# Modulation weights in halves with their four products together, a bank for the value block's last turn, and the turn of dt one z block later

## The chip, the cores and the metric

The kernel runs on one core of one Trainium2 chip. The metric is device time in microseconds (us). The kernel before was run three times: 1810.01, 1811.7 and 1812.62 us, median 1811.7.

## The reference

A two-layer backbone over 1024 latent tokens and 256 context tokens of width 1024, in float32. Layer 0 feeds one projection into a bidirectional RG-LRU and a differential attention with four heads; layer 1 is a bidirectional Mamba-2 (SSD). Around each layer stands an adaptive modulation, and that is what most of the change is about:

```python
def modulation(cvec, w, b):                      # w: 1024 x 3072, one per layer
    m = jax.nn.silu(cvec) @ w + b
    return jnp.split(m, 3, axis=-1)
...
sh, sc, gt = modulation(c, w_mod[i], b_mod[i])   # latent tokens
sh_c, sc_c, gt_c = modulation(c_ctx, w_mod[i], b_mod[i])   # context tokens
u_lat = rms_norm(h_lat, g_pre[i]) * (1.0 + sc[:, None]) + sh[:, None]
...
h_lat = h_lat + gt[:, None] * rms_norm(y_lat, g_post[i])
```

So two vectors, silu(c) and silu(c_ctx), are multiplied by a 1024 x 3072 matrix in each layer. The shift and scale (the first 2048 columns) are needed ahead of a layer, the gate (the last 1024) behind it.

## The kernel before

**Engines and order.** Each engine works through its own instructions in order. A planner sorts each engine's instructions ahead of time, by the order of the program and by its own estimate of when things are ready. `tc.issue_after(x)` adds an edge to it: what is inside the block comes behind x on its engine. TensorE runs everything that is a product; ScalarE (ACT) and VectorE (DVE) empty its PSUM banks; loads are issued from SP's and ScalarE's queues. Float32 products are made exact enough by splitting both operands in a high and a low part, so each projection matmul comes three times (wh x uH, wl x uH, wh x uL: `proj`, L321). A projection block is 128 output columns of a weight by 1280 tokens, in slices of 512, 512 and 256 tokens, 72 matmuls.

**The modulation products.** The two silu vectors stand as the first two of 32 columns of `silu_c` (the rest is zero), eight k tiles of 128. For each k tile there are four products, j = 0 to 3, each of 512 weight columns, into partitions 32j to 32j+31 of one PSUM bank; the profile shows such a float32 product as two matmul records. Three places do this:

- `modulation` (L135) for layer 0, at the start of the kernel: in two passes of 256-column products; the weights of a k tile come in one load of 512 KB that holds all four products' columns.
- `gate_rows` (L187): the gate columns of both layers. Each of the four products of a k tile has a weight tile and a load of its own (256 KB, 2 KB per partition), from a pool `wmod1` of five such buffers. Afterwards the four rows (two silu vectors each) go through the same steps one after the other: VectorE copies the row from PSUM (L199), loads b_mod's part (L203, issued by ScalarE's queue), adds it, loads g_post's part into the same kind of buffer, multiplies (L204), and stores the row to memory (L205, SP's queue). Row and b_mod/g_post parts have one buffer each (tags `u` and `gbm`).
- `modulation` for layer 1: the same with 512-column products, four loads of 256 KB per k tile from the same pool; then ScalarE copies the bank to `mrow` (L165; the buffer with tag `u` of gate_rows), and four transposes turn it.

In program order (L1360 to L1384): LRU block 0's and 1's projections, the scan of block 0, gate_rows, block 2's projections, the scan of block 1, modulation of layer 1, then the weight pool and its small pool close and their memory goes to the rope tables, whose loads (L1366) are issued by ScalarE's queue; then block 3's projections, the scan of block 2, and the first query, gate and key blocks of attention, of which query and key need the rope tables.

**Fills.** `fill` issues matmuls of the identity whose result is not used, behind the last TensorE instruction. `FILL[3]` is 1; it stands in front of the first value transposes.

**The value block's turn.** `v_block` (L471) projects the values of a head and turns ten 128 x 128 tiles by transposes in groups of 4, 4 and 2, each group in a PSUM bank from `c.psum`; for head "0" this pool has two banks, so the third group takes the bank of the first, behind the copy that empties it (L484).

**dt's turn.** In `layer1` (L786) the step sizes dt are worked out by `dt_block`; `turn()` makes the products that transpose and sum them. It stands behind the last matmul of z block 0 (an `issue_after` edge).

Of the kernel before, what the change touches and what calls it, by code (L numbers as in the profile page):

```python
# [10 lines left out]
F32 = mybir.dt.float32  # L11
# [8 lines left out]
P = 128  # L20
D = 1024
KT = 8
# [12 lines left out]
FILL = (5, 1, 1, 1, 1)  # L35
# [96 lines left out]
    return ab  # L132


def modulation(c, a, layer, wpool, tmp, ahead=None, between=None):  # L135
    nc = c.nc
    pcol = 16 if layer == 0 else 93
    gcol = 40 if layer == 0 else 117
    ms = c.cst.tile([P, 16, 2], F32, name=f"ms{layer}")
    g = c.cst.tile([P, KT, 2], F32, name=f"g{layer}")  # L140
    parts = 2 if between else 1
    kn = KT // parts
    nq = kn // 2
    cw = nq * P
    for hf in range(parts):
        pm = c.pm()
        for k in range(KT):
            src = a["w_mod"][layer, k * P : (k + 1) * P, 0 : 2 * D].rearrange("p (s d) -> p s d", s=2)
            cols = []
            if parts == 2:  # L150
                wm = wpool.tile([P, 2, 512], F32, name=f"wm{layer}_{hf}{k}", tag="wm")
                nc.sync.dma_start(wm, src[:, :, 512 * hf : 512 * hf + 512])
                cols = [wm[:, 0, :], wm[:, 1, :]]
            else:
                for j in range(4):
                    wm = wpool.tile([P, cw], F32, name=f"wm{layer}_{j}{k}", tag="wm")
                    nc.sync.dma_start(wm, src[:, j // 2, cw * (j % 2) : cw * (j % 2) + cw])
                    cols.append(wm)
            if ahead:
                ahead(hf, k)  # L160
            for j in range(4):
                w = cols[j // 2][:, cw * (j % 2) : cw * (j % 2) + cw] if parts == 2 else cols[j]
                nc.tensor.matmul(pm[32 * j : 32 * j + 32, 0:cw], c.sc[:, k, :], w, start=(k == 0), stop=(k == KT - 1))
        mrow = tmp.tile([P, 512], F32, name=f"mrow{layer}{hf}", tag="u")[:, 0:cw]
        nc.scalar.copy(mrow, pm[:, 0:cw])  # L165
        pc = c.pm()
        if layer == 0:
            fill(c, pc, FILL[1], cw)
        for q in range(nq):
            nc.tensor.transpose(pc[:, P * q : P * q + P], mrow[:, P * q : P * q + P], c.ident)  # L170
        if layer == 0 and hf == 0:
            c.turned = last_pe(nc)
        pv = pc[:, 0:cw].rearrange("p (q j r) -> p j q r", q=nq, r=32)
        for h in range(2):
            o = 8 * h + kn * hf
            nc.vector.tensor_tensor(ms[:, o : o + kn, :].rearrange("p (j q) s -> p j q s", q=nq), pv[:, 2 * h : 2 * h + 2, :, 0:2],
                                    c.pa[:, pcol + o : pcol + o + kn].rearrange("p (j q) -> p j q", q=nq).unsqueeze(3).to_broadcast([P, 2, nq, 2]), OP.add)
        ks = slice(kn * hf, kn * hf + kn)
        nc.vector.scalar_tensor_tensor(g[:, ks, :], ms[:, 8 + ks.start : 8 + ks.stop, :], 1.0,
                                       c.pa[:, gcol + ks.start : gcol + ks.stop].unsqueeze(2).to_broadcast([P, kn, 2]),  # L180
                                       OP.add, OP.mult)
        if between and hf == 0:
            between(ms, g)
    return ms, g


def gate_rows(c, a, wpool, tmp):  # L187
    nc = c.nc
    pm = c.pm()
    for k in range(KT):  # L190
        for j in range(4):
            w = wpool.tile([P, 512], F32, name=f"wg{j}_{k}", tag="wm")
            o = 2 * D + 512 * (j % 2)
            nc.sync.dma_start(w, a["w_mod"][j // 2, k * P : (k + 1) * P, o : o + 512])
            nc.tensor.matmul(pm[32 * j : 32 * j + 32, :], c.sc[:, k, :], w, start=(k == 0), stop=(k == KT - 1))
    for j in range(4):
        layer, n = j // 2, slice(512 * (j % 2), 512 * (j % 2) + 512)
        row = tmp.tile([P, 512], F32, name=f"grow{j}", tag="u", bufs=1)[0:2, :]
        nc.vector.tensor_copy(row, pm[32 * j : 32 * j + 2, :])  # L199
        for q, src, op in ((0, a["b_mod"][layer : layer + 1, 2 * D + n.start : 2 * D + n.stop], OP.add),  # L200
                           (1, a["g_post"][layer : layer + 1, n], OP.mult)):
            bm = tmp.tile([2, 512], F32, name=f"gbm{j}{q}", tag="gbm", bufs=1)
            nc.scalar.dma_start(bm, src.to_broadcast([2, 512]))  # L203
            nc.vector.tensor_tensor(row, row, bm, op)  # L204
        nc.sync.dma_start(c.grow_d[:, layer, n], row)  # L205

# [17 lines left out]
def last_pe(nc):  # L224
    return next(i for i in reversed(nc.cur_bb.bb.instructions) if i.engine == mybir.EngineType.PE)


def fill(c, ps, n, w=512, behind=None):

    nc = c.nc  # L230
    with c.tc.issue_after(behind or last_pe(nc)):
        for _ in range(n):
            nc.tensor.matmul(ps[:, :w], c.ident, c.ident.unsqueeze(1).to_broadcast([P, w // P, P]), start=True, stop=True)
# [239 lines left out]
def v_block(c, w, uH, uL, pool, apool, name):  # L473
    nc = c.nc
    vt = pool.tile([P, T], F32, name=f"vt_{name}", tag="qf")
    proj(c, w, uH, uL, name, lambda ps, t0, n: nc.scalar.copy(vt[:, t0 : t0 + n], ps))
    v = apool.tile([P, NT, P], F32, name=f"v_{name}", tag="v", bufs=2)
    for j0, n in ((0, 4), (4, 4), (8, 2)):
        ps = c.psum()
        if name == "0" and j0 == 0:  # L480
            fill(c, ps, FILL[3])
        for j in range(n):
            nc.tensor.transpose(ps[:, j * P : (j + 1) * P], vt[:, (j0 + j) * P : (j0 + j + 1) * P], c.ident)
        nc.scalar.copy(v[:, j0 : j0 + n, :], ps[:, : n * P].rearrange("p (j e) -> p j e", e=P))  # L484
    return v
# [304 lines left out]
def layer1(c, a, uH, uL, U, out, dram, h_d, psm, xdt):  # L790
    nc, tc = c.nc, c.tc
# [14 lines left out]
    zp = c.upool  # L806
    nz = 3
    with ExitStack() as s1:
        pool = s1.enter_context(tc.tile_pool(name="p1", bufs=2, side="right"))
        c.wpools = [(U.enter_context(tc.tile_pool(name=f"wst1{i}", bufs=1)), U.enter_context(tc.tile_pool(name=f"wsp1{i}", bufs=1))) for i in range(2)]  # L810
        c.wcyc = 0
        with tc.tile_pool(name="dtp", bufs=1, side="right") as dp:
            tabs, turn = dt_block(c, a, xdt, dp, scst, dr)
            z_block(c, a, 0, uH, uL, zp, dr)
            with tc.issue_after(c.last):
                turn()
        for i in range(1, nz):
            z_block(c, a, i, uH, uL, zp, dr)
        late, store = [None], []

        def block(i, slices, done):
            x = conv_block(c, a, i, uH, uL, pool, slices, late[0])
            late[0] = done(x)

        for g in range(G):
            def done_b(xb, g=g):
                nc.scalar.dma_start(dr["bt"][g], xb[:, 259:XC])
                return lambda: nc.scalar.dma_start(dr["bk"][g], tok_major(c, xb, pool, f"b{g}"))

            def done_c(xc, g=g):  # L830
                nc.scalar.dma_start(dr["ct"][g], xc[:, 259:XC])

            block(16 + g, SL1, done_b)
            block(20 + g, SLAT, done_c)
            for q in range(4):
                def done_x(xs, g=g, q=q):
                    def tok():
                        t = tok_major(c, xs, pool, f"x{4 * g + q}")
                        nc.scalar.dma_start(dr["xk"][g, :, :, q * P : (q + 1) * P].rearrange("c p e -> p c e"), t[:, 2:, :])
                        while store:  # L840
                            store.pop()()
                        store.append(x_states(c, t, 4 * g + q, pool, tabs[0], dr))
                    return tok

                block(4 * g + q, SL1, done_x)
        z_block(c, a, nz, uH, uL, zp, dr)
        with tc.issue_after(c.last):
            late[0]()
        store.pop()()
# [3 lines left out]
    k = ssd_setup(c, a, dr, tabs, S, psm)  # L853
# [5 lines left out]
    for i in range(nz + 1, 16):  # L859
# [4 lines left out]
        n = i - nz - 2  # L864
# [338 lines left out]
def backbone(ctx, tc, a, out):  # L1203
    nc = tc.nc
    c = Ctx()
# [3 lines left out]
    dr = {}  # L1209
# [22 lines left out]
    uH = upool.tile([P, KT, T], F32R, name="u0H")  # L1232
    uL = upool.tile([P, KT, T], F32R, name="u0L")
# [109 lines left out]
    cur = lru_in(c, a, 0, lp, qp, uH, uL, rest)  # L1343
    s4 = ExitStack()
    sp1 = c.sp1
    wm = s4.enter_context(tc.tile_pool(name="wmod1", bufs=5))
    tmp = s4.enter_context(tc.tile_pool(name="mtmp1", bufs=1))
    for i in range(4):
        nxt = lru_in(c, a, i + 1, lp, qp, uH, uL) if i < 3 else None
# [196 lines left out]
```

## Time and profile before

The page is of one profiled execution on the chip. Engines' busy times are shares of its span; the span is the time between its first and last recorded instruction.

| | |
|---|---|
| time of the profiled execution | 1812.95 us |
| its span | 1811.0 us |
| mean granted TensorE clock | 0.991 of full speed |
| TensorE (PE) busy | 97%, 8896 matmuls |
| VectorE (DVE) / ScalarE (ACT) / GpSimd (POOL) busy | 61% / 43% / 20% |
| read / written in device memory | 165.99 MB / 78.92 MB |

A row of a timeline gives the start and length of one instruction or of several alike (x8), its engine, line and operation, the tile that it writes and those that it reads, and in brackets how long the engine stood idle before it and what ended that. PEclk is the granted clock of TensorE as a share of 2.4 GHz. Matmul records overlap, since the array is pipelined: their lengths add up to more than the time that they take.

### The profile page before, as it was taken

Reading aid. Unit: us, or ns where it says so; the run is one execution under the profiler, and the core shown is the slowest. Engines: PE = TensorE matmul, PEld = TensorE weight load, DVE = VectorE, ACT = ScalarE, POOL = GpSimd, SP = SyncE. Lnnn points to the kernel's source line nnn. Section 1 sums busy time; section 2 is a strip of 40 time slices with the busy share of each in tenths; the row PEclk is TensorE's granted clock in tenths of the full one; section 3 lists DMA queues with packets and bytes.
Section 4 is the critical chain, followed back from the end, with each engine's and each line's share of the span. In section 5 each row is a group of like instructions: output and inputs, shape, how many; then the busy total and the mean of one; then the engine's idle time right before and its main releaser. Section 6 shows DMA issues by size and latency. Waiting matters only on the chain.

```text
span 1811.0 us, 24076 instructions
## 1 busy us (share of the span) xinstructions
PE 1753.4 (97%) x8896; PEld 1327.8 (73%) x8896; DVE 1106.3 (61%) x1646; ACT 782.1 (43%) x1571; POOL 369.0 (20%) x423
## 2 busy tenths in 40 slices
PE   6999999999999998999999999999999999999997
PEld 2665377788888887886788888887777566666675
DVE  3735456784837667566746565655111766777797
ACT  4542455374636456444433333334111554343443
POOL 1201000000000000110005242424111443434432
PEclk9999999999999999999999999999999999999999
DMA  7434513432222225342335353546632655656464
GB/s 249 147 97 154 172 64 124 140 86 90 78 75 70 85 53 189 117 140 82 89 121 148 114 145 123 148 124 178 216 105 82 221 194 176 223 193 210 157 206 146
DMA packets 231290, 250.42 MB, mean 138 GB/s; under 512 B 16329, under 2 KB 176078, under 8 KB 231174
## 3 DMA queue, kind: packets, MB, share of 16 engines
q1 hardware_dynamic: 202416, 217.12, 38.5%
q10 hardware_dynamic: 28758, 31.78, 5.5%
q8 instruction: 70, 1.15, 0.3%
q14 instruction: 46, 0.38, 0.1%
HBM read 165.99 MB, written 78.92 MB: 135 GB/s over the span
## 4 chain that ended last, share of the span: by engine, by line
PE 43%; DVE 5%; ACT 2%; issue 1%; DMA 1%; POOL 1%; ACTq 0%; DVEq 0%; SPq 0%; POOLq 0%
PE psap L321 13%; PE pscp L321 11%; PE psap L1119 8%; PE psat L929 3%; PE psdo L1061 2%; PE psdy L1083 2%; PE psda L1050 1%; DVE xbc L350 1%; PE psdy L1078 1%; DVE wl_xb L299 1%; PE psda L1034 1%; PE pscu L747 0%; ACT xp_xb L340 0%; PE psat L1111 0%; ACT tok_x L748 0%
## 5 line engine op out<-in xcount | busy, mean ns | idle before, releaser
L768 POOL TENSOR_TENSOR x2w<-tok_x,wd 128x1152 f32<-128x1152 f32 (+2 forms) x48 | 119.3, 2511 | 108.4 <-issue 61.9
L350 DVE SCALAR_TENSOR_TENSOR xbc<-xp_xb,pb,xbc 128x1283 f32<-128x1283 f32 (+1 forms) x72 | 132.7, 1843 | 3.0
L940 POOL TENSOR_TENSOR s<-s,etb 128x512 f32<-128x512 f32 x64 | 75.1, 1175 | 215.1 <-DVE s L941 102.3
L1119 PE MATMUL psap<-wo1h,yh 128*128 128x512 f32 x256 | 114.0, 446 | 0.0
L348 DVE TENSOR_SCALAR xbc<-xp_xb,pb 128x1283 f32<-128x1283 f32 (+1 forms) x24 | 22.2, 926 | 133.1 <-ACT xp_xb L340 96.4
L1119 PE MATMUL psap<-wo1l,yh 128*128 128x512 f32 x256 | 102.3, 399 | 0.2
L941 DVE TENSOR_TENSOR s<-s,psat 128x512 f32<-128x512 f32 x64 | 43.5, 680 | 94.2 <-PE psat L929 94.0
L1119 PE MATMUL psap<-wo1h,yl 128*128 128x512 f32 x256 | 101.0, 394 | 0.0
L321 PE MATMUL pscp<-u1H,wh_xb 128*128 128x512 f32 x232 | 92.7, 399 | 0.0
L321 PE MATMUL pscp<-u1H,wl_xb 128*128 128x512 f32 x232 | 92.6, 399 | 0.0
L321 PE MATMUL pscp<-u1L,wh_xb 128*128 128x512 f32 x232 | 92.4, 398 | 0.0
L623 POOL TENSOR_TENSOR ors<-z,mhalf 128x4 f32<-128x4 f32 (+1 forms) x12 | 13.7, 1146 | 382.3 <-DVE z L621 315.7
L321 PE MATMUL psap<-u1H,wh_z 128*128 128x512 f32 x208 | 86.3, 415 | 0.0
L321 PE MATMUL psap<-u1H,wl_z 128*128 128x512 f32 x208 | 83.1, 400 | 0.0
L585 ACT ACTIVATE p<-scores,nm 128x1024 f32<-128x1024 f32 x64 | 71.5, 1117 | 25.3 <-DVE nm L584 16.1
L321 PE MATMUL psap<-u1L,wh_z 128*128 128x512 f32 x208 | 82.2, 395 | 0.0
L560 PE MATMUL scores<-kk,xq 128*128 128x512 f32 (+1 forms) x208 | 76.3, 379 | 2.8 <-ACT p L585 2.6
L1050 PE MATMUL psda<-At,Rt 128*128 128x512 f32 x128 | 76.7, 602 | 1.0 <-DVE psda L1052 0.9
L736 ACT ACTIVATE xbc<-xbc 128x1283 f32<-128x1283 f32 (+1 forms) x24 | 29.8, 1241 | 106.0 <-DVE xbc L350 106.0
L929 PE MATMUL psat<-x,bk 128*128 128x512 f32 x144 | 74.2, 597 | 0.6 <-DVE s L941 0.6
L561 PE MATMUL scores<-kk,xl 128*128 128x512 f32 (+1 forms) x208 | 71.7, 359 | 0.0
L612 PE MATMUL psat<-v,wT 128*128 128x128 f32 x572 | 71.4, 278 | 0.0
(484 smaller groups left out, 4983.5 us busy)
## 6 DMA issues: line engine op xcount, KB each, us to landing
d_x<-x2w SPq DMA_DIRECT2D x32, 576.0 KB
x<-d_x SPq DMA_DIRECT2D x72, 256.0 KB
wst_xb<-in_o_w_in_dram SPq DMA_DIRECT2D x24, 512.0 KB
d_acc<-acc SPq DMA_DIRECT2D x24, 512.0 KB
acc<-d_acc SPq DMA_DIRECT2D x24, 512.0 KB
wm<-in_w_mod_dram SPq DMA_DIRECT2D x16, 512.0 KB
wg<-in_w_mod_dram SPq DMA_DIRECT2D x32, 256.0 KB
wm<-in_w_mod_dram SPq DMA_DIRECT2D x32, 256.0 KB
```

Source lines behind the costliest of these rows:

```text
L321: nc.tensor.matmul(ps[:n, :w_], l[:, k, :], r[:, k, t0 : t0 + w_], start=(k == 0 and i == 0), stop=(k == KT - 1 and i == 2))
L350: nc.vector.scalar_tensor_tensor(out[:, j0 : j0 + n], xp[:, j0 + k : j0 + k + n], cw(k), out[:, j0 : j0 + n], OP.mult, OP.add)
L560: nc.tensor.matmul(out, xq[m][:, qs], kk[m][:, k0 : k0 + n], start=True, stop=False)
L561: nc.tensor.matmul(out, xl[:, m, qs], kk[m][:, k0 : k0 + n], start=False, stop=True)
L585: nc.scalar.activation(pr[m][:, NCTX:], scores[m], AF.Exp, bias=nm[:, m : m + 1], accum_out=zz[:, 1, m : m + 1])
L612: nc.tensor.matmul(po[:, :P], wT[:, j, :], v[:, j, :], start=(j == 0), stop=(j == nkt - 1))
L768: nc.gpsimd.tensor_tensor(x2[:, o : o + n, :].rearrange("p c (h e) -> p c h e", e=64), t[:, a0:a1, :].rearrange("p c (h e) -> p c h e", e=64),
L929: nc.tensor.matmul(ps, self.bk[g][:, t, :], x2, start=True, stop=True)
L940: nc.gpsimd.tensor_tensor(sn, self.prev[g, d], self.et[:, hs, t : t + 1].to_broadcast([P, 8, 64]), OP.mult)
L941: nc.vector.tensor_tensor(sn, sn, psv, OP.add)
L1050: nc.tensor.matmul(pa, R[:, d, :], A[:, 4 * hh : 4 * hh + 4, :].rearrange("p h l -> p (h l)"), start=True, stop=True)
L1119: nc.tensor.matmul(po, l[:, q, :], w[:, n], start=(q == 0 and i == 0), stop=(q == 3 and i == 2))
```

## The change

`together` is new: it issues product 2, and then the other three directly behind it. All three places of the modulation products use it. In gate_rows and in layer 1 the weights now come in halves: two loads of 512 KB per k tile, each with two products' columns, from a pool of three buffers of 4 KB per partition (before: five of 2 KB). The gate rows go in eight pieces of 256 columns, and a piece, its b_mod part and its g_post part share one tile with one buffer. The one identity matmul of FILL[3] moves from the value block to the second pass of layer 0's modulation. The third group of value transposes of head "0" takes a bank from `c.pm`, the pair of banks that the modulation used. And dt's turn stands behind z block 1 instead of z block 0.

```diff
--- before.py
+++ after.py
@@ -132,6 +132,13 @@
     return ab
 
 
+def together(c, product):
+    product(2)
+    with c.tc.issue_after(last_pe(c.nc)):
+        for j in (3, 0, 1):
+            product(j)
+
+
 def modulation(c, a, layer, wpool, tmp, ahead=None, between=None):
     nc = c.nc
     pcol = 16 if layer == 0 else 93
@@ -152,15 +159,17 @@
                 nc.sync.dma_start(wm, src[:, :, 512 * hf : 512 * hf + 512])
                 cols = [wm[:, 0, :], wm[:, 1, :]]
             else:
-                for j in range(4):
-                    wm = wpool.tile([P, cw], F32, name=f"wm{layer}_{j}{k}", tag="wm")
-                    nc.sync.dma_start(wm, src[:, j // 2, cw * (j % 2) : cw * (j % 2) + cw])
+                for i in range(2):
+                    wm = wpool.tile([P, D], F32, name=f"wm{layer}_{i}{k}", tag="wm")
+                    nc.sync.dma_start(wm, src[:, i, :])
                     cols.append(wm)
             if ahead:
                 ahead(hf, k)
-            for j in range(4):
-                w = cols[j // 2][:, cw * (j % 2) : cw * (j % 2) + cw] if parts == 2 else cols[j]
-                nc.tensor.matmul(pm[32 * j : 32 * j + 32, 0:cw], c.sc[:, k, :], w, start=(k == 0), stop=(k == KT - 1))
+            def product(j):
+                nc.tensor.matmul(pm[32 * j : 32 * j + 32, 0:cw], c.sc[:, k, :], cols[j // 2][:, cw * (j % 2) : cw * (j % 2) + cw],
+                                 start=(k == 0), stop=(k == KT - 1))
+
+            together(c, product)
         mrow = tmp.tile([P, 512], F32, name=f"mrow{layer}{hf}", tag="u")[:, 0:cw]
         nc.scalar.copy(mrow, pm[:, 0:cw])
         pc = c.pm()
@@ -170,6 +179,8 @@
             nc.tensor.transpose(pc[:, P * q : P * q + P], mrow[:, P * q : P * q + P], c.ident)
         if layer == 0 and hf == 0:
             c.turned = last_pe(nc)
+        elif layer == 0:
+            fill(c, c.pm(), FILL[3])
         pv = pc[:, 0:cw].rearrange("p (q j r) -> p j q r", q=nq, r=32)
         for h in range(2):
             o = 8 * h + kn * hf
@@ -188,19 +199,25 @@
     nc = c.nc
     pm = c.pm()
     for k in range(KT):
-        for j in range(4):
-            w = wpool.tile([P, 512], F32, name=f"wg{j}_{k}", tag="wm")
-            o = 2 * D + 512 * (j % 2)
-            nc.sync.dma_start(w, a["w_mod"][j // 2, k * P : (k + 1) * P, o : o + 512])
-            nc.tensor.matmul(pm[32 * j : 32 * j + 32, :], c.sc[:, k, :], w, start=(k == 0), stop=(k == KT - 1))
-    for j in range(4):
-        layer, n = j // 2, slice(512 * (j % 2), 512 * (j % 2) + 512)
-        row = tmp.tile([P, 512], F32, name=f"grow{j}", tag="u", bufs=1)[0:2, :]
-        nc.vector.tensor_copy(row, pm[32 * j : 32 * j + 2, :])
+        wm = []
+        for layer in range(2):
+            w = wpool.tile([P, D], F32, name=f"wg{layer}_{k}", tag="wm")
+            nc.sync.dma_start(w, a["w_mod"][layer, k * P : (k + 1) * P, 2 * D : 3 * D])
+            wm.append(w)
+        def product(j):
+            nc.tensor.matmul(pm[32 * j : 32 * j + 32, :], c.sc[:, k, :], wm[j // 2][:, 512 * (j % 2) : 512 * (j % 2) + 512],
+                             start=(k == 0), stop=(k == KT - 1))
+
+        together(c, product)
+    for j, o in ((j, o) for j in range(4) for o in (0, 256)):
+        layer, n = j // 2, slice(512 * (j % 2) + o, 512 * (j % 2) + o + 256)
+        t = tmp.tile([P, 512], F32, name=f"grow{j}{o}", tag="u", bufs=1)
+        row = t[0:2, 0:256]
+        nc.vector.tensor_copy(row, pm[32 * j : 32 * j + 2, o : o + 256])
         for q, src, op in ((0, a["b_mod"][layer : layer + 1, 2 * D + n.start : 2 * D + n.stop], OP.add),
                            (1, a["g_post"][layer : layer + 1, n], OP.mult)):
-            bm = tmp.tile([2, 512], F32, name=f"gbm{j}{q}", tag="gbm", bufs=1)
-            nc.scalar.dma_start(bm, src.to_broadcast([2, 512]))
+            bm = t[0:2, 256:512]
+            nc.scalar.dma_start(bm, src.to_broadcast([2, 256]))
             nc.vector.tensor_tensor(row, row, bm, op)
         nc.sync.dma_start(c.grow_d[:, layer, n], row)
 
@@ -476,9 +493,7 @@
     proj(c, w, uH, uL, name, lambda ps, t0, n: nc.scalar.copy(vt[:, t0 : t0 + n], ps))
     v = apool.tile([P, NT, P], F32, name=f"v_{name}", tag="v", bufs=2)
     for j0, n in ((0, 4), (4, 4), (8, 2)):
-        ps = c.psum()
-        if name == "0" and j0 == 0:
-            fill(c, ps, FILL[3])
+        ps = c.pm() if name == "0" and j0 == 8 else c.psum()
         for j in range(n):
             nc.tensor.transpose(ps[:, j * P : (j + 1) * P], vt[:, (j0 + j) * P : (j0 + j + 1) * P], c.ident)
         nc.scalar.copy(v[:, j0 : j0 + n, :], ps[:, : n * P].rearrange("p (j e) -> p j e", e=P))
@@ -811,10 +826,11 @@
         c.wcyc = 0
         with tc.tile_pool(name="dtp", bufs=1, side="right") as dp:
             tabs, turn = dt_block(c, a, xdt, dp, scst, dr)
-            z_block(c, a, 0, uH, uL, zp, dr)
+            for i in range(2):
+                z_block(c, a, i, uH, uL, zp, dr)
             with tc.issue_after(c.last):
                 turn()
-        for i in range(1, nz):
+        for i in range(2, nz):
             z_block(c, a, i, uH, uL, zp, dr)
         late, store = [None], []
 
@@ -1343,7 +1359,7 @@
     cur = lru_in(c, a, 0, lp, qp, uH, uL, rest)
     s4 = ExitStack()
     sp1 = c.sp1
-    wm = s4.enter_context(tc.tile_pool(name="wmod1", bufs=5))
+    wm = s4.enter_context(tc.tile_pool(name="wmod1", bufs=3))
     tmp = s4.enter_context(tc.tile_pool(name="mtmp1", bufs=1))
     for i in range(4):
         nxt = lru_in(c, a, i + 1, lp, qp, uH, uL) if i < 3 else None
```

## Rows read from the trace of the kernel before

**Rows 1.** the page, parts 1 and 4: TensorE; the chain by engine.

```profile
PE 1753.4 (97%) x8896; PEld 1327.8 (73%) x8896; DVE 1106.3 (61%) x1646; ACT 782.1 (43%) x1571; POOL 369.0 (20%) x423
PE 43%; DVE 5%; ACT 2%; issue 1%; DMA 1%; POOL 1%; ACTq 0%; DVEq 0%; SPq 0%; POOLq 0%
```

**Rows 2.** windows: us, busy of PE, PEld, DVE, ACT, POOL; PEclk, DMA, GB/s.

```profile
120.00:165.00 45.00, 45.00 (x156) 17.09 (x155) 17.17 (x13) 17.51 (x20) 4.83 (x5) 1.00 0.64 199
180.00:230.00 50.00, 49.96 (x175) 19.45 (x174) 20.07 (x18) 21.53 (x25) 4.18 (x6) 1.00 0.52 158
```

**Rows 3.** windows, products (L195, L163) alone: PE, PEld, PEclk, DMA, GB/s.

```profile
121.09:163.85 42.76, 22.53 (x64) 3.17 (x64) 1.00 0.65 203
182.07:228.55 46.48, 23.80 (x64) 3.35 (x64) 1.00 0.56 170
```

**Rows 4.** timeline of PE around single and grouped products.

```profile
139.19 0.40 PE L321 MATMUL psbp<-u0L,wh_xr 128*128 128x512 f32 x1
139.52 1.04 PE L195 MATMUL psat<-wg,silu_c 128*32 128x512 f32 x2
140.50 0.49 PE L321 MATMUL psbp<-u0H,wh_xr 128*128 128x512 f32 x1
140.83 0.39 PE L321 MATMUL psbp<-u0H,wl_xr 128*128 128x512 f32 x1
141.06 0.40 PE L321 MATMUL psbp<-u0L,wh_xr 128*128 128x512 f32 x1
...
184.10 1.06 PE L163 MATMUL psbm<-wm,silu_c 128*32 128x512 f32 x8
```

**Rows 5.** timeline of the gate rows' pieces: VectorE and the DMA queues.

```profile
163.96 0.68 DVE L199 COPY grow<-psat 2x512 f32<-2x512 f32 x1 [9.87 <-PE psat L195]
185.03 0.40 ACTq L203 DMA_DIRECT2D gbm<-in_g_post_dram  x1
187.47 0.68 DVE L204 TENSOR_TENSOR grow<-grow,gbm 2x512 f32<-2x512 f32 x1 [1.05 <-DMA gbm<-in_g_post_dram]
190.38 0.26 SPq L205 DMA_DIRECT2D d_grow<-grow  x1
192.74 0.69 DVE L199 COPY grow<-psat 2x512 f32<-2x512 f32 x1 [4.58 <-DMA d_grow<-grow]
203.89 0.29 SPq L205 DMA_DIRECT2D d_grow<-grow  x1
```

**Rows 6.** timeline at the end of layer 1's modulation and the first query block.

```profile
228.66 0.59 ACT L165 COPY mrow<-psbm 128x512 f32<-128x512 f32 x1 [1.45 <-PE psbm L163]
230.65 0.36 ACTq L1366 DMA_DIRECT2D ropeC_s<-in_ropeC_dram  x1
245.14 0.68 PE L321 MATMUL psbp<-u0H,wh_q 128*128 128x256 f32 x1
```

**Rows 7.** timeline of the value block's transposes and copies.

```profile
320.38 1.02 PE L233 MATMUL psbt<-ident 128*128 128x512 f32 x2
321.23 1.04 PE L483 MATMUL psbt<-ident,vt 128*128 128x128 f32 x8
332.54 1.49 ACT L484 COPY v<-psbt 128x512 f32<-128x512 f32 x3 [6.99 <-DVE sh_q L462]
333.18 0.44 PE L483 MATMUL psbt<-ident,vt 128*128 128x128 f32 x2 [2.57 <-ACT v L484]
```

**Rows 8.** windows, columns as in rows 2, with TensorE below full clock.

```profile
57.00:61.00 4.00, 3.94 (x16) 2.94 (x15) 3.29 (x6) 3.48 (x6) 2.43 (x3) 0.57 0.32 79
330.00:338.00 8.00, 5.43 (x18) 4.04 (x17) 2.58 (x5) 1.45 (x3) 0.00 (x0) 0.79 0.75 205
900.00:908.00 8.00, 8.00 (x35) 6.03 (x34) 2.54 (x6) 1.53 (x2) 0.00 (x0) 0.57 0.20 45
```

**Rows 9.** timeline of PE after layer 0's second transposes.

```profile
55.98 0.39 PE L321 MATMUL psbp<-u0H,wh_xr 128*128 128x256 f32 x1 [1.17 <-ACT u0H L259]
```

**Rows 10.** timeline of PE at dt's turn.

```profile
898.39 0.83 PE L716 MATMUL pscu<-ident,rmask 64*128 64x64 f32 x10 [1.30 <-ACT rmask L701]
```

## The prediction, made before the changed kernel was built or run

> **What bounds the kernel now.** I read the page's busy shares first, then the chain of waits by engine, then tables by stretch of the span, then the order of instructions on each engine. TensorE is busy 97% of the span, and the chain that ended last is for the most part TensorE [rows 1]. So a microsecond of TensorE's time saved anywhere is worth about a microsecond, if no wait takes its place. In the two stretches where the modulation products run (gate_rows from 121 us, modulation of layer 1 from 182 us) TensorE has no idle time at all, at 2.4 GHz (PEclk 1.00), while VectorE and ScalarE are below half [rows 2]. These stretches are bound by TensorE's order of work.
>
> What TensorE does there is the point. Each product has 32 output columns (half of its rows are padding), two matmul records of 512 columns. The products' records cover 22.53 us of the first stretch and 23.80 us of the second [rows 3], for 32 products each. A product alone covers 1.04 us and holds the engine from 139.52 to 140.50; four started back to back cover 1.06 us in all [rows 4]. So the array runs the four beside each other, and a visit of one costs what a visit of four costs. 46.33 us at 1.05 is 44 visits, where 16 (eight k tiles, twice) would do.
>
> **The products, together.** Price of a visit: from the projection matmul before it to the one after it 1.31 us (139.19 to 140.50) where two projection matmuls are otherwise 0.23 apart (140.83 to 141.06), so 1.08; and the one after it holds the engine 0.33 instead of 0.23, another 0.10 [rows 4]. Together 1.18 us. The order constraint issues product 2, which waits for the later of the two halves, and then the other three with nothing left to wait for. 44 - 16 = 28 visits fewer at 1.18 us: **-33.0 us**. Bounds: 32 visits, if each k tile splits in two (12 fewer, -14.2), and -33.0. Layer 0's products mostly stand in fours already; what is split there lies ahead of the wait for x and is counted at nothing.
>
> The Trainium skill (TensorE: Matmul & The Clock Gate, section "Measured speedup vs the span model") gives 3.07 times for four packed tiles and 2.38 times for three by columns, so by an estimate from it four together cost 4/3.07 = 1.30 of one. The trace differs, 1.06 against 1.04 [rows 4], and the measurement decides; by the page the sixteen visits would cost 16 x 0.3 = 4.8 us more, and the sum would be 1789.
>
> **Halves in three buffers.** Bytes stay the same; 64 issues of 256 KB become 32 of 512 KB. Two buffers hold one k tile and the third half of the next, so each group of four waits for one half that could only be issued after the group before it. A round trip: a small load takes 2.44 us from its issue to the instruction that it releases (185.03 to 187.47) [rows 5], and 512 KB at the stretch's mean of 203 GB/s [rows 3] 2.6 us more, then the group itself: at most 6.1 us. Before, a k tile took 42.76/8 = 5.35 us. I leave the end of gate_rows where it is, 163.9 us. That wait costs TensorE nothing as long as projection matmuls of the next LRU blocks fill it: about 4 us, 18 matmuls at 0.23, for each group, and there are two blocks of 72 and the scan's products in each stretch. Behind a waiting product stands everything on TensorE, which is in order; SP's queue holds the weight blocks behind these loads. If the planner puts too few matmuls between groups the cover is gone; that is a rival below.
>
> **The gate rows in eight pieces.** This edit speaks against the change. A row piece, its bias and its gain now share one tile with one buffer: per piece, load the bias, add, load the gain, multiply, store, and only then may the next piece begin. That is three DMA legs where a piece had two (the next bias was loaded beside the store), and eight pieces instead of four. Legs: load 2.44; store 2.36 (190.38 to 192.74) [rows 5]. With two short VectorE operations of about 0.4 (half of the 0.68 that 512 columns took [rows 5]) a piece is 2 x 2.44 + 2.36 + 0.8 = 8.0 us, the copy being hidden beside the first load. Waits in the three queues come on top: the four pieces of before ran from 163.96 to 203.89 + 2.36, 10.6 each, against 2.44 + 2.36 + 3 x 0.68 = 6.8 worked out the same way. Most of that was VectorE and SP standing behind late TensorE work, which the change removes; I take 8.5 us, with 7.4 (legs of 2.2) and 13.5 (the slowest piece of before, 192.74 to 206.2) as the ends.
>
> Who waits: layer 1's mrow copy takes the same buffer. It started at 228.66 when the products were done, 22 us after the last store; the rope tables' loads stand behind it (230.65) [rows 6], because their memory is that of the pool that closes there. Now the copy waits for 163.9 + 8 x 8.5 = 232. TensorE reaches the first query block at 245.14 - 33 = 212 [rows 6] and can run its 72 matmuls (48 x 0.23 + 24 x half of that, 13.8 us) and some 4 us of the scan's, until both projection banks wait for the rope: at 230. It resumes 2.0 us (228.66 to 230.65), a 512 KB load of about 4.3 (between 2.44 + 1.5 and 5.0) and a shuffle of 0.7 after the copy starts, so at 239. In general the stall is 8p - 59 us for a piece of p: 9 us here, nothing at 7.4, 49 at 13.5. After an idle stretch TensorE has run at 1.2 GHz for 3.4 us or more (rows at PEclk 0.57 and 0.79 [rows 8]), another 1.7 lost. **+10.7 us.**
>
> **A bank for the value block's last turn.** The last two transposes wait 2.57 us for a copy at 332.54, and everything on TensorE stands behind them [rows 7]. With a bank of their own they follow the first eight at once. The stretch 330 to 338 has PEclk 0.79, so 3.4 us at 1.2 GHz [rows 8], 1.7 us lost; the fill in front of the transposes (320.38 to 321.23) leaves too, 0.85. Next in line are the query and key blocks of the second head, with banks free. **-5.1 us**; ends: 0 (the wait moves to the next bank user) and -5.1.
>
> The fill moves behind layer 0's second transposes, where TensorE waits 1.17 us for ScalarE [rows 9]: 0.85 hidden there, at worst 0.85 in the open. It could keep the clock up in 57 to 61 us, where TensorE spends 3.4 us at 1.2 GHz and so loses 1.7, but VectorE and ScalarE are busy 82 and 87% there [rows 8] and feed TensorE: between -1.7 and 0, taken as 0.
>
> **dt's turn.** It waits 1.30 us at 898.39 for ScalarE's exponential [rows 10]. By that time all three z blocks and 50 matmuls of the next block have been issued, so that the turn already stands later than the new edge asks for; no DMA is in it, and queued behind it are the convolution matmuls. I take 0. If it did move away from its wait, 1.3 and the 3.4 us that 6.8 us at 1.2 GHz cost in 900 to 908 [rows 8] would go: -4.7. If the VectorE copies of wd come later: +1.3.
>
> **Sum.** The profiled execution took 1812.95 us (span 1811.0 and 1.95 around it): 1812.95 - 33.0 - 5.1 + 10.7 = 1785.6. The median of the runs shown is 1.25 lower: **1784 us**. Attention and layer 1 are TensorE bound too, so what is saved before 340 us is kept.
>
> **Rivals.**
> 1. No stall: a piece takes 7.4 us or TensorE finds other work. For it: nothing but these small transfers is then on ScalarE's and SP's queues for long. Against: 10.6 per piece before. 1784 - 10.7 = 1773.
> 2. The products don't come together: scan matmuls are earlier in the program and cut in, two visits per k tile. For it: modulation of layer 1 begins with such cuts. Gain 14.2 + 5.1; TensorE then arrives later, and the stall goes: 1811.7 - 19.3 = 1792.
> 3. The weights become the wait. If, as now, only some ten matmuls (2.3 us) lie between four products while a half needs 2.4 + 1.5 = 3.9 us, each of 14 groups waits 1.6 us: 22 us back; TensorE's lead shrinks to 11, without the other stall: 1811.7 - 33.0 - 5.1 + 22 = 1796.
> 4. Slower: the eight pieces become the bound of the stretch. At 13.5 us a piece, mrow starts at 272, TensorE stands still for 49 us and the scan behind it with it: 1811.7 - 38.1 + 49 + 1.7 = 1824. From 12 us a piece on nothing is left of the gain. For it: three queues in order, with loads of 512 KB ahead of each store. Against: only one piece of before was that slow.
>
> **Chances.** My forecast 0.42, rival 1 0.22, rival 2 0.11, rival 3 0.12, rival 4 0.10, dt or others 0.03. Within 0.2% (3.6 us, about what a measurement of this kernel tells from no change) only a piece of 11.6 to 12.5 us lands: 0.04, taken half from rival 4's lower end. Faster 0.87, same 0.04, slower 0.09. The likeliest case's own range is 1777 to 1793 (a piece of 7.6 to 9.6 us); the range for 8 in 10 takes in rivals 1 to 3 and the lower part of 4: 1771 to 1806.
>
> **What would show it.** In each of the two stretches the products stand in eight groups, x8 in the timeline, and their records cover about 8.5 us (8 x 1.06) instead of 22.5 and 23.8. The q block's first matmul near 212. mrow's copy late, released by a store of a row piece, and TensorE idle before the first gd block until the rope product. No wait at the value block's transposes. The turn of dt where it was, some 30 us earlier. The forecast is wrong if the groups are cut, if idle time ahead of product records appears with the weights as releaser, or if the pieces take over 12 us.

## The result, and the profile after

The changed kernel takes 1788.76 us (median of four runs, 1786.44 to 1792.54) against 1811.42 us in the same comparison: ratio 0.9877, 95% interval 0.9858 to 0.9896, 22.7 us less. Beside the experiments below it was timed again on one chip: 1788.25 against 1814.51 us, ratio 0.9862 (0.9843 to 0.988). The forecast was 1784 us, in a range of 1771 to 1806. The profiled execution took 1792.54 us, the slowest of the four; its span is 1790.7 us.

TensorE is no longer without idle time where the products run. The page and the same windows as in [rows 3], the products' lines alone (us, busy of PE and PEld, PEclk, DMA share, GB/s):

```profile
PE 1725.9 (96%) x8896; PEld 1327.1 (74%) x8896; DVE 1108.1 (62%) x1658; ACT 780.9 (44%) x1571; POOL 374.5 (21%) x423
```

```profile
119.97:156.77 36.80, 9.56 (x64) 1.38 (x64) 1.00 0.66 220
171.16:209.34 38.18, 10.60 (x64) 1.52 (x64) 1.00 0.61 197
```

The same 64 records cover 9.56 and 10.60 us where they covered 22.53 and 23.80 [rows 3]. By the starts of the records there are 9 visits and 10, where the same count gives 20 and 22 before (the forecast's 44 is the cover divided by that of one product; a visit of more than four products covers more, 1.90 us for five). Most k tiles stand as x8; three are split, one product being left behind a few matmuls of the scan. But now a group of four waits for its weights. TensorE's timeline from one group to the next:

```profile
136.54 1.07 PE L208 MATMUL psbm<-wg,silu_c 128*32 128x512 f32 x8 [0.90 <-DMA wg<-in_w_mod_dram]
137.54 0.50 PE L338 MATMUL psbp<-u0H,wh_xr 128*128 128x512 f32 x1
...
140.17 0.39 PE L338 MATMUL psbp<-u0L,wh_xr 128*128 128x512 f32 x1
141.50 1.07 PE L208 MATMUL psbm<-wg,silu_c 128*32 128x512 f32 x8 [0.94 <-DMA wg<-in_w_mod_dram]
```

Twelve projection matmuls stand between (12 to 21 at the ten groups that wait), and ten such waits of 0.46 to 0.94 us add up to 7.6 us.

Then the gate rows. Their eight pieces, layer 1's mrow, the rope tables and TensorE behind them, in order of time (in brackets idle time and what ended it):

```profile
156.86 0.41 DVE L216 COPY grow<-psbm 2x256 f32<-2x256 f32 x1 [1.84 <-PE psbm L208]
219.13 0.50 PE L338 MATMUL psbp<-u0H,wh_gr 128*128 128x512 f32 x1 [1.98 <-DVE sg_gr L375]
234.29 0.43 DVE L216 COPY grow<-psbm 2x256 f32<-2x256 f32 x1 [2.31 <-DMA d_grow<-grow]
242.03 0.25 SPq L222 DMA_DIRECT2D d_grow<-grow  x1
244.51 0.57 ACT L174 COPY mrow<-psat 128x512 f32<-128x512 f32 x1
246.20 0.36 ACTq L1382 DMA_DIRECT2D ropeC_s<-in_ropeC_dram  x1
253.47 0.67 DVE L478 TENSOR_TENSOR q_q<-psbp,ropeC_s 128x512 f32<-128x512 f32 x1
254.19 0.58 PE L338 MATMUL psbp<-u0H,wh_gd 128*128 128x256 f32 x1 [4.79 <-DVE q_q L478]
```

The reader is to see the last store at 242.0, mrow's copy only after it though the products ended at 209, the rope behind mrow, and TensorE idle for 4.79 us. The value block and dt's turn, by TensorE's timeline:

```profile
303.00 1.27 PE L498 MATMUL psbt<-ident,vt 128*128 128x128 f32 x8
304.11 0.38 PE L498 MATMUL psat<-ident,vt 128*128 128x128 f32 x2
...
876.63 0.83 PE L731 MATMUL pscu<-ident,rmask 64*128 64x64 f32 x10 [1.30 <-ACT rmask L716]
```

The last two transposes follow the first eight without a wait; dt's turn waits the same 1.30 us as in [rows 10], behind the same 50 matmuls of the next block.

A measure that the later parts don't disturb is the time from the first gate product of the LRU (line of `bdr`) to the first product of attention (`scores`): 116.44 to 345.01 us before, 115.31 to 323.81 after, so 228.6 and 208.5 us, 20.1 less. It is given for each experiment, from one profiled execution each ("by the trace" below). It holds gate_rows, layer 1's modulation and the value block, but neither layer 0's modulation nor dt's turn. The spans of the two profiled executions differ by 20.3 us; of the 22.7 us between the medians the rest is not located.

### The profile page after: what moved, and what is told of

The parts are those of the page before. It is cut to its first block, busy times and chain, and to the rows that moved or that the text cites. A ratio compares the mean times of both kernels' runs of the same rounds, so it can differ in the third digit from the quotient of the medians.

```text
span 1790.7 us, 24043 instructions
## 1 busy us (share of the span) xinstructions
PE 1725.9 (96%) x8896; PEld 1327.1 (74%) x8896; DVE 1108.1 (62%) x1658; ACT 780.9 (44%) x1571; POOL 374.5 (21%) x423
## 4 chain that ended last, share of the span: by engine, by line
PE 44%; DVE 5%; ACT 2%; DMA 1%; issue 1%; POOL 1%; ACTq 0%; DVEq 0%; POOLq 0%; SPq 0%
PE psap L338 14%; PE pscp L338 11%; PE psap L1135 8%; PE psat L945 3%; PE psdo L1077 2%; PE psdy L1099 2%; PE psda L1066 1%; DVE xbc L367 1%; PE psdy L1094 1%; DVE wl_xb L316 1%; PE psda L1050 1%; PE pscu L762 0%; ACT xp_xb L357 0%; PE psat L1127 0%; ACT tok_x L763 0%
```

## The experiments

Ratios are to the kernel before, with 95% intervals. The kernel before had a median of 1814.51 us in the first comparison (four kernels on one chip) and 1809.93 us in the second, so ratios are compared, not times of the two.

**The changed kernel again.** 

> The changed kernel once more, beside the others on one chip. Every theory expects 0.987 of the time before, about 1788 us, and it shows whether 1.2 GHz windows of the changed kernel's profile (10.24 us at dt's turn, where before had 6.83) belong to it or to that execution: if they belong to it, the window is 10.24 us again.

1788.25 us, ratio 0.9862; first attention product after 208.8 us, 0.3 more than in the first profile, though of the two stretches at 1.2 GHz there, 3.41 us each from 219.7 and from 253.8, only the second is back. At dt's turn the two executions differ (window of the first, then of this one; PEclk is the third figure from the end):

```profile
876.00:884.00 8.00, 7.37 (x40) 5.63 (x41) 3.40 (x7) 3.62 (x6) 0.00 (x0) 0.66 0.30 70
```

```profile
876.00:884.00 8.00, 7.47 (x51) 5.83 (x52) 3.31 (x7) 3.53 (x6) 0.00 (x0) 1.00 0.31 70
```

The same kernel ran once with and once without the stretch at 1.2 GHz, so it belongs to the execution and is not to be explained by the change.

**Without the order edge.**

```diff
-    product(2)
-    with c.tc.issue_after(last_pe(c.nc)):
-        for j in (3, 0, 1):
-            product(j)
+    for j in range(4):
+        product(j)
```

> The changed kernel without the order edge: products 0 to 3 in program order, the planner free to part them; halves, buffers and all else as changed. In its order of instructions the products then stand in some 28 groups, mostly pairs, where the changed kernel has 19 and the kernel before 44 visits. Theory 1 (a visit costs 1.18 us whatever stands in it; the edge, not the halves, brings four together): 9 more visits, 10.6 us, less what the pairs hide of the 7.6 us that the groups of four wait for weights: 1792 to 1799 us. Rival (fewer and larger loads are the gain, the edge adds nothing): 1788 us, as changed. Rival (only whole groups of four pay): 1811 us.

1791.53 us, ratio 0.9875 (0.9861 to 0.9889); 211.3 us to the first attention product. The products stand in 27 visits, mostly pairs (x4), and only one of them waits for weights (0.47 us):

```profile
190.97 1.05 PE L167 MATMUL psat<-wm,silu_c 128*32 128x512 f32 x4
191.95 0.50 PE L336 MATMUL psbp<-u0H,wh_xr 128*128 128x512 f32 x1
...
193.76 1.05 PE L167 MATMUL psat<-wm,silu_c 128*32 128x512 f32 x4
```

The records of the products cover 30.14 us instead of 20.16. With 0.13 us for entry and exit (1.18 less 1.05) of eight visits more that is 11.0 us, and 7.1 of the 7.6 us of waits are gone: 3.9 us by this account, 2.5 to 2.8 by the trace. The intervals of the two ratios overlap, so the times alone don't tell theory 1 from a gain of nothing by the edge; the rival of 1811 us is out. By starts, 15 of the 23 visits saved are saved without the edge; the edge takes away the last eight and pays for most of them in waits.

**The edge without the halves.**

```diff
-            w = wpool.tile([P, D], F32, name=f"wg{layer}_{k}", tag="wm")
+            w = wpool.tile([P, 512], F32, name=f"wg{j}_{k}", tag="wm")
...
-    wm = s4.enter_context(tc.tile_pool(name="wmod1", bufs=3))
+    wm = s4.enter_context(tc.tile_pool(name="wmod1", bufs=5))
```

> The edge without the halves: the changed kernel with the weights again in quarters of 256 KB from five buffers, and four products still together (the quarter that is loaded last leads). Only one quarter of the next k tile can be loaded before a group is done. Theory 1 (each group then waits for a round trip: 2.44 us of latency and 768 KB at 203 GB/s, 3.8 us, plus the group's own 1.0, so 7.2 us a k tile, of which the order fills about 15 matmuls, 3.5 us): some 2.7 us of waiting in 14 groups against 0.8 now, 27 us more, about 1815 us. Rival (the queue's rate sets the pace, 1 MB in 4.9 us however it is cut): 1789 us with waits of 0.8 as in the changed kernel.

1798.85 us, ratio 0.9925 (0.9907 to 0.9944); 215.8 us to the first attention product. Groups stand together (19 visits), and ten waits for weights take 13.6 us, 0.87 to 1.72 each:

```profile
150.61 1.06 PE L209 MATMUL psbm<-wg,silu_c 128*32 128x512 f32 x8 [1.72 <-DMA wg<-in_w_mod_dram]
157.40 1.07 PE L209 MATMUL psbm<-wg,silu_c 128*32 128x512 f32 x8 [1.57 <-DMA wg<-in_w_mod_dram]
...
260.29 0.58 PE L339 MATMUL psbp<-u0H,wh_gd 128*128 128x256 f32 x1 [7.65 <-DVE q_q L479]
```

The direction is theory 1's, the size about a third: 7.0 to 7.3 us more by the trace and some 9 to 11 by the ratios, where 27 were forecast. A k tile takes 5.6 to 7.8 us between two waiting groups, 6.4 in the mean, where 7.2 were worked out, and the planner puts 15 to 24 matmuls between, so that a wait is about 1.4 us and not 2.7. The rival, with waits of 0.8 us and 1789 us, falls. The row pieces start later (at 166.4 us, not 156.9) and layer 1's mrow is copied later (250.1, not 244.5); the wait at the gd block is 7.65 us.

**The third group's bank back.**

```diff
-        ps = c.pm() if name == "0" and j0 == 8 else c.psum()
+        ps = c.psum()
```

> The changed kernel with the value block's third group of transposes back in the pool of two banks. Theory 1 (the wait for the copy, 2.57 us in the kernel before, and the 1.2 GHz window behind it, 1.7 us lost, come back): about 1792.5 us, 4 more than changed, and TensorE idle ahead of the last two transposes. Rival (the wait was only the place where TensorE met VectorE's and ScalarE's lag, which the changed kernel meets elsewhere, at 254 us): within 1 us of the changed kernel.

1794.63 us, ratio 0.989 (0.9876 to 0.9904), 6.4 us over the changed kernel; 211.7 us to the first attention product, 2.8 to 3.2 more. The wait is back, with 3.41 us at 1.2 GHz behind it (from 315.5):

```profile
315.01 0.44 PE L498 MATMUL psbt<-ident,vt 128*128 128x128 f32 x2 [2.08 <-ACT v L499]
```

So the rival, which expected no more than 1 us, falls by the trace.

**Gate rows without the serial chain.**

```diff
+    t = wpool.tile([P, D], F32, name="grow", tag="wm")
+    row, gain = t[:, 0:512], t[:, 512:D]
+    bias = tmp.tile([P, 512], F32, name="gbias", tag="u", bufs=1)
...
+        nc.vector.tensor_tensor(row[r, :], pm[r, :], bias[r, :], OP.add)
+        nc.vector.tensor_tensor(row[r, :], row[r, :], gain[r, :], OP.mult)
+        nc.sync.dma_start(c.grow_d[:, layer, n], row[r, :])
```

> The changed kernel with another chain of gate rows: bias and gain of all four rows are loaded ahead into buffers of their own (gain and rows in one weight buffer), then two VectorE operations a row and a store, nothing serial. Theory 1 (the serial chain of eight pieces, 156.9 to 242.0 us in the trace, holds VectorE 11.5 us in front of copies, layer 1's mrow copy, the rope tables and so TensorE, which waits 1.98 us at 219.13 and 4.79 us at 254.19, each followed by 3.41 us at 1.2 GHz): both waits go, up to 6.8 + 2 x 1.7 = 10 us less, 1779 to 1782 us. Rival (VectorE's scans of block 2, which stand ahead of the rope product in its order, set the wait at 254.19): no more than 2 us less, 1786 to 1788 us, and a wait of some 4 us stays ahead of the gd block.

1786.24 us, ratio 0.986 (0.9838 to 0.9882), 2.0 us less by the medians; 204.9 us to the first attention product, 3.6 to 3.9 less. The rows' last store is issued at 161 us, mrow's copy starts at 210.7, and the waits for q_q and sg_gr are gone. But TensorE stops at the same block all the same:

```profile
257.12 0.50 PE L339 MATMUL psbp<-u0H,wh_gd 128*128 128x512 f32 x1 [3.04 <-DVE sg_gd L376]
```

This is what the rival expected, with another releaser. VectorE's order ahead of it shows why:

```profile
251.68 2.32 DVE L455 TENSOR_TENSOR_SCAN a<-r,a,T 128x1024 f32<-128x1024 f32 x1
253.92 1.15 DVE L481 TENSOR_TENSOR q_q<-q_q,sh_q 128x512 f32<-128x512 f32 x1
254.99 1.74 DVE L459 TENSOR_TENSOR a<-a,a 128x1024 f32<-128x1024 f32 x1
256.66 0.41 DVE L376 SCALAR_TENSOR_TENSOR sg_gd<-th_gd,psbp 128x256 f32<-128x256 f32 x1
```

The scans of block 2 stand ahead of the copy that frees gd's bank. The kernel before had this very wait, with the same order on VectorE:

```profile
279.17 0.79 PE L321 MATMUL psbp<-u0H,wh_gd 128*128 128x512 f32 x1 [3.06 <-DVE sg_gd L358]
```

So the chain of rows did not add 4.79 us there; it put 4.79 in the place of 3.06. How much of the 3.6 to 3.9 us is the chain's is open. Against the first profile of the changed kernel the weights' waits are 1.3 us longer and all other waits 1.7 shorter, which nearly cancel; what is left is the two stretches at 1.2 GHz, 1.7 us each, which this execution does not have (its window behind the wait of 3.04 us, PEclk third from the end):

```profile
257.00:262.00 5.00, 4.88 (x21) 4.05 (x22) 4.33 (x5) 4.90 (x6) 0.00 (x0) 1.00 0.95 373
```

The kernel before had such a stretch behind the same wait.

**Seven quarters, rows apart.** The weights in quarters as in the run without the halves, the rows without the chain; rows, gain, bias and mrow take buffers of the weights' pool:

```diff
-    wm = s4.enter_context(tc.tile_pool(name="wmod1", bufs=3))
-    tmp = s4.enter_context(tc.tile_pool(name="mtmp1", bufs=1))
+    wm = s4.enter_context(tc.tile_pool(name="wmod1", bufs=7))
```

> Seven quarters of 256 KB in place of three halves (the rows and layer 1's mrow take buffers of the same pool, bias and gain apart as in the run before), four products together: three quarters of the next k tile lie ready, one is to come. Theory 1 (the waits for weights, ten of about 0.8 us in the changed kernel, go and are worth their time): 8 us below the kernel with the rows apart, about 1778 us. Rival (TensorE arrives earlier and waits the longer at the gd block, where VectorE's part of the scan, the releaser sg_gd after 3.04 us with the rows apart, sets the time): 1786 us, with a wait of 6 us or more at the gd block.

1782.63 us, ratio 0.9851 (0.9827 to 0.9874), the lowest median of all; its interval overlaps the changed kernel's, so the times alone don't settle that it beats it. By the trace the first attention product comes after 200.3 us, 4.6 below the rows apart and 8.2 to 8.5 below the changed kernel. The rival falls: the wait at the gd block is 3.05 us as before, not 6. But theory 1 has the wrong cause. The waits did not go, 7.1 us in ten (8.9 with the rows apart), since the planner now puts about ten matmuls (9 to 13) between groups:

```profile
138.43 1.06 PE L209 MATMUL psbm<-wg,silu_c 128*32 128x512 f32 x8 [0.43 <-DMA wg<-in_w_mod_dram]
...
142.73 1.06 PE L209 MATMUL psbm<-wg,silu_c 128*32 128x512 f32 x8 [0.74 <-DMA wg<-in_w_mod_dram]
```

There are 16 visits instead of 19, one of them of six products (1.91 us). The records' cover falls by 2.3 us (20.17 to 17.88), three entries and exits at 0.13 are 0.4, weights' waits are 1.8 us less and the other waits 1.7 less; one stretch of 3.41 us at 1.2 GHz, from 253.8, costs 1.7 that the rows apart did not pay: 4.5 in all against 4.6 measured. The kernel with the lowest median so far loads its weights in quarters, so larger loads are not what brings the gain. Five quarters took 215.8 us by the trace and seven, with the rows apart, 200.3: that it is the buffers for the next k tile is likely, but the rows were not changed by themselves.

**Seven quarters with the chain.** One buffer of the weights' pool for all eight pieces, and none shared with mrow, which so no longer waits for the chain; the rope tables, which take the pool's memory, still do.

```diff
-    bias, gain = (wpool.tile([P, 512], F32, name=f"grow{q}", tag="wm") for q in "bg")
+    t = wpool.tile([P, 512], F32, name="grow", tag="wm")
```

> The seven quarters with the changed kernel's serial chain of eight row pieces (in one buffer of the pool): weights' waits away, chain as changed. Theory 1 (the chain costs what the run with the rows apart showed, 2 to 4 us, whatever stands ahead): 2 to 4 us over the seven quarters with rows apart. Rival (the chain has a fixed end, near 244 us in the trace, so what TensorE saves ahead of it is lost in waiting for the rope): no faster than the changed kernel, 1787 to 1789 us, with some 12 us of waiting ahead of the gd block.

1788.64 us, ratio 0.9871 (0.9851 to 0.9892); 202.7 us to the first attention product, 2.4 over the rows apart. The sum is theory 1's, but it is not the chain's price alone: the products now stand in 18 visits and not 16, their cover 2.1 us longer. The medians, 6 us apart, would also fit the rival. Its mechanism isn't there: TensorE waits 2.11 and 3.21 us ahead of the gd block, not 12, and the chain has no fixed end. Its last store is issued at 225.3, 17 us earlier than in the changed kernel, and mrow is copied at 206.4, ahead of it; the rope loads are issued from 227.6, behind it.

**Fill and dt's turn back.**

```diff
-        elif layer == 0:
-            fill(c, c.pm(), FILL[3])
...
-            for i in range(2):
-                z_block(c, a, i, uH, uL, zp, dr)
+            z_block(c, a, 0, uH, uL, zp, dr)
             with tc.issue_after(c.last):
                 turn()
```

> The changed kernel with two of its small parts undone: the identity matmul of the fill back in front of the value transposes and out of layer 0's modulation, and dt's turn back behind z block 0. Theory 1 (0.85 us of a fill that is in the open at the value block, hidden in layer 0; dt's place in TensorE's order unchanged): 0 to 1 us over the changed kernel, and the first product of dt's turn behind 50 matmuls of the next block as before. Rival (the fill in layer 0 keeps TensorE at full clock there, where the kernel before ran 3.41 us at 1.2 GHz from 57.3 us and the changed one did not): that window comes back and 1.7 us with it, 1790 us or more.

1790.28 us, ratio 0.9883 (0.9865 to 0.9902), overlapping the changed kernel's; 207.5 us to the first attention product, 1.0 to 1.3 less, not more, for which no row gives a cause. TensorE again waits 1.17 us in layer 0 (0.31 with the fill there), and the granted clock is full from 57 to 61 us all the same, so the rival about the clock falls:

```profile
55.48 0.39 PE L336 MATMUL psbp<-u0H,wh_xr 128*128 128x256 f32 x1 [1.17 <-ACT u0H L274]
...
876.21 0.83 PE L731 MATMUL pscu<-ident,rmask 64*128 64x64 f32 x10 [1.40 <-ACT rmask L716]
```

The first product of dt's turn stands behind 50 matmuls of the next block in all three kernels. Neither part does anything that these times can tell.

## Why the prediction came out right, and where its terms were off

- **A visit costs what it holds the array, not what is in it.** Right, up to four products. Counted as the forecast does (44 to 19), 25 visits fewer at 1.18 us are 29.5 us (forecast 28, -33.0); three k tiles still split in two, which rival 2 had for all of them. A group covers 1.06 us (9.56 in nine visits), a product alone 1.04 [rows 4]. The runs with 27 and 16 visits agree with this price to 1.4 us or better once cover and waits (and, with 16 visits, the clock) are counted. The 1.30 of one product that the forecast estimated from the Trainium skill (TensorE: Matmul & The Clock Gate, "Measured speedup vs the span model"), from its figure for four tiles packed by rows, isn't seen here; by that estimate 19 visits would have been some 6 us dearer.
- **"That wait costs TensorE nothing."** This step failed. 18 matmuls per group were counted as cover and the order has 12 in most places, so a loop of 4.6 to 5.0 us (141.50 less 136.54 is 4.96; at most 6.1 was worked out) waits about 0.8 us. The term 0 measures +7.6 us: rival 3 in part, at half its 1.6 us per group. Together the products bring -21.9 us.
- **The rows' chain.** The mechanism is as told, to the mrow copy, the rope and the idle TensorE, but the term +10.7 was too large. The pieces were slower than the 8.5 us assumed: from the first copy at 156.86 to mrow's copy at 244.51 are eight pieces of 11.0 (VectorE's part of a piece stands in its queue behind the scan, as in the last piece, whose bias addition starts at 238.97 us for a load issued at 234.29). By the formula 8p - 59 that would be 29 us. But the chain began 7 us earlier than the 163.9 that was kept for it, and TensorE came to the query block at 228.9 and not at 212 (for the most part waits, split tiles, the wait at 219). With both put in, the formula gives 4.7, and 4.79 was measured; that close is in part luck, since TensorE both stopped and went on 2.7 us later than the formula has it. Two more things were missed: the wait of 1.98 us at the gr block, and the 3.06 us of waiting that stood at the gd block already. The wait that a new one replaces has to be subtracted. Taking the chain away brought 3.6 to 3.9 us by the trace, of which the 1.2 GHz stretches that were missing there can be the most; the pair with seven quarters (2.4) differs in its visits too.
- **The value block.** -5.1 forecast; undoing the bank alone costs 2.8 to 3.2 us by the trace and 6.4 by the medians. Right in its wait and the 1.2 GHz behind it.
- **Fill and dt's turn.** 0 and 0, and the medians overlap; the turn stood behind 50 matmuls of the next block before and after, as the forecast says.

The account to the first attention product: visits -29.5, waits for weights +7.6, waits at the gr and gd blocks 4.79 + 1.98 - 3.06 = +3.7, 1.2 GHz behind them (two stretches of 3.41 us, one before) +1.7, the value block's wait, clock and fill -5.1: -21.6, measured -20.1; 1.5 us are not assigned. Against the forecast's -27.4 the waits are +7.6 and the visits +3.5, and the rows' chain, 5.4 with its clock instead of 10.7, is -5.3: errors of 16.4 us in all leave 5.8 in the sum. The sum was better than its terms, which is luck: the waits that were left out and the rows' chain, at twice its size, erred in opposite directions. And each 1.2 GHz stretch of 3.41 us that comes or goes shifts such an account by 1.7 us.

## What to carry to other kernels

Where small products run beside each other on the array, count visits, and buy the grouping with buffers: a group that needs a whole k tile must find enough of the next tile loaded, or it hands the gain to the load's round trip. Before a new wait is priced, look for the wait that already stands at that point; only the difference is paid. And two changes that save the same visits, a coarser tile and an order edge, don't add: without the edge 15 visits were saved, without the halves 23, with both 23.

## What the runs showed of the hardware

The same kernel differs between executions by which stretches run at 1.2 GHz. With the rows apart, five executions took 1784.8 to 1795.8 us; the fastest had a mean granted clock of 0.994 and the slowest 0.988, and 0.6% of 1790 us is 10.7 us, nearly the whole difference of 11.0. Two executions of the same 1786.24 us had 0.992 and 0.994, so the mean clock does not settle every difference. A wait of TensorE of about 3.05 us at the gd block had a stretch of 3.41 us at 1.2 GHz behind it in the kernel before and with seven quarters, and none with the rows apart. Effects of 2 or 3 us were read from the distance between two rows of a trace, not from medians; two executions of the changed kernel differ by 0.3 us in that distance, and every other kernel was traced once.
